# Splitting the rows of the first load of a max-pooling kernel into 8 KB pieces

## The chip, the cores and the metric

The kernel runs on one core of one Trainium2 chip. The metric is the device time of one execution in microseconds (us), lower is better. A time is a median over runs; a profile is one further execution, recorded by the hardware profiler.

## The reference

The input `x` has the shape (32, 256, 4096) in float32, and the output has 256 values for each of the 32 x 256 rows. As 4096 is divisible by 256, this is a maximum over every 16 neighbouring elements:

```python
for i in range(output_size):          # output_size = 256
    start = int(i * length / output_size)
    end = int((i + 1) * length / output_size)
    result[:, :, i] = np.max(x[:, :, start:end], axis=-1)
```

It reads 134.2 MB and writes 8.4 MB. There is one comparison for each element read and nothing else to compute.

## The kernel before

The kernel sees `x` as a list of 2,097,152 windows of 16 floats (64 bytes). The windows are dealt to the 128 partitions in two contiguous groups: group a gives each partition 15,436 windows that follow each other in memory, group b another 948. Within a group, partition p holds one unbroken stretch, so one load takes one contiguous row from each partition's stretch: a load of 1,024 windows is 128 rows of 64 KB.

The loads, in the order in which SyncE (SP) issues them:

- load 0, 1,024 windows a partition (8.4 MB, line 96): "the long first load";
- a load of 128 windows (`FIRST`, 1 MB in 128 rows of 8 KB, line 87), which has no number of its own;
- loads 1 to 13, 1,024 windows each (line 96);
- load 14 with 972 windows and load 15, which is group b, with 948 (line 96).

All loads go to one queue (q1), whose packets are carried by sixteen DMA engines; each load of 128 rows gives each engine eight rows. In the profile a row is one packet, and each engine adds one small packet at the end of a transfer for its completion.

The buffer `ring` holds two slots of 1,024 + 152 windows (`CHUNK` and `GAP`). Even loads go to the first slot, odd loads to the second, and within its slot every second load is moved up by 152 windows:

```python
low = n_loads % 2 * (CHUNK + GAP)
moved = n_loads // 2 % 2
at = low + moved * GAP
nc.sync.dma_start(out=ring[:, at * W : (at + n) * W], in_=xn)
```

So load 0 lies at windows 0 to 1,023, the 128-window load in 1,024 to 1,151, load 1 at 1,176 to 2,199, load 2 at 152 to 1,175, load 3 at 1,328 to 2,351, load 4 at 0 to 1,023 again. VectorE (DVE) reduces each load with `reduce_max` (helper `pooled`, line 56) in two parts: first the 872 windows that the slot's next load will overwrite, then the other 152. The next load into that slot can be issued when the part of 872 is done. Load 2 is the exception: it lies over the 128-window load's place too, so it waits for three reductions, of 872, 152 and 128 windows. VectorE works in the order of the program.

The framework places the waits: SP waits, before each issue from load 2 on, for the reduction that frees the place, and VectorE waits for each load's landing. SP issues in the order of the program, so an issue that waits holds up those behind it.

The results of group a gather in `kept` and are stored once, at the end, by SP (line 116). The last load's results overwrite a part of `ring` and are stored by ScalarE's queue (q10, line 113).

Of the kernel before, what the change touches and what calls it, by code (L numbers as in the profile page):

```python
# [1 line left out]

# [4 lines left out]


@with_exitstack
def kernel(  # L10
    ctx: ExitStack,
    tc: tile.TileContext,
    x: bass.AP,
    output_size: bass.AP,
    out: bass.AP,
):

    nc = tc.nc
    P = nc.NUM_PARTITIONS
    fp32 = mybir.dt.float32

    B, C, L = x.shape
    O = int(output_size)  # L30
    assert L % O == 0, (L, O)
    W = L // O
    total = B * C * O // P
    assert B * C * O % P == 0

    CHUNK = 1024
    GAP = 152
    FIRST = 128
    LOADS = 14

    last = 948
    group_a = [total - last - LOADS * CHUNK - FIRST] + [CHUNK] * LOADS
    group_a.insert(-1, FIRST)
    group_b = [last]
    assert FIRST < group_a[0] <= CHUNK and last * (W + 1) <= CHUNK * W

    pool = ctx.enter_context(tc.tile_pool(name="pool", bufs=1))
    ring = pool.tile([P, 2 * (CHUNK + GAP) * W], fp32, tag="ring", name="ring")
    kept = pool.tile([P, total - last], fp32, tag="kept", name="kept")

    xw = x.flatten_outer_dims().rearrange("r (o w) -> (r o) w", w=W)
    ow = out.flatten_outer_dims().rearrange("r o -> (r o)")

    def pooled(dst, at, n):

        nc.vector.reduce_max(  # L56
            out=dst,
            in_=ring[:, at * W : (at + n) * W].rearrange("p (n w) -> p n w", w=W),
            axis=mybir.AxisListType.X,
        )  # L60

    taken = 0

    def group(n):

        nonlocal taken
        span = slice(taken * P, (taken + n) * P)
        taken += n
        return (
            xw[span].rearrange("(p n) w -> p (n w)", p=P),  # L70
            ow[span].rearrange("(p n) -> p n", p=P),
        )

    stores = []
    n_loads = 0
    base = 0
    for g, loads in enumerate((group_a, group_b)):
        xg, og = group(sum(loads))
        a = sum(loads) if g == 0 else 0
        for n in loads[::-1]:  # L80
            if g == 0:
                a -= n
            xn = xg[:, a * W : (a + n) * W]
            dst = kept[:, base + a : base + a + n] if n != last else None
            if n == FIRST:

                nc.sync.dma_start(  # L87
                    out=ring[:, CHUNK * W : (CHUNK + n) * W], in_=xn
                )
                pooled(dst, CHUNK, n)  # L90
            else:

                low = n_loads % 2 * (CHUNK + GAP)
                moved = n_loads // 2 % 2
                at = low + moved * GAP
                nc.sync.dma_start(out=ring[:, at * W : (at + n) * W], in_=xn)  # L96
                if n != last:
                    cut = CHUNK - GAP if moved else GAP
                    parts = [(0, cut), (cut, n)]
                    for u, v in parts if moved else parts[::-1]:  # L100
                        pooled(dst[:, u:v], at + u, v - u)
                else:
                    end = (at + CHUNK) * W
                    last_kept = ring[:, end - n : end]
                    pooled(last_kept, at, n)
                n_loads += 1
            if g:
                a += n
        if g == 0:
            stores.append((og, kept[:, :]))  # L110
    assert taken == total

    nc.scalar.dma_start(out=og, in_=last_kept)
    tc.no_sync_barrier()
    for dst, src in stores:
        nc.sync.dma_start(out=dst, in_=src)


# [1 line left out]
_INS = ['x', 'output_size']  # L120
_OUTS = [((32, 256, 256), 'float32')]

_NUMBERS = {'output_size': 256}


# [26 lines left out]
```

## Time and profile before

| what | value |
|---|---|
| median of 3 runs | 337.88 us (337.59 to 338.27) |
| time of the profiled execution | 338.23 us |
| its span, first to last instruction | 336.4 us |
| busy time of VectorE | 276.5 us, 82% of the span |
| packets on the load queue q1 | 2,592, 142.12 MB, 98.2% of sixteen engines' span |
| mean DMA rate over the span | 424 GB/s |
| full reduction of 872 windows | 14.7 us, 15 times |
| issue of load 0 | at 0.73 us, takes 0.37 |
| issue of the 128-window load, of load 1 | at 1.15 us (0.43), at 1.62 us (0.42) |
| issue of load 2 | at 42.30 us, takes 0.33 |

The span is the time from the first to the last instruction; the execution's own time is 1.8 us longer, for what lies around it. All start times are counted from the start of the span. In a timeline line the columns are the start, the duration, the engine and line, the operation, output and input, and in brackets the engine's idle time before and what ended it; neighbouring instructions are merged into one line (x2, x3). In a table of windows the columns are the stretch, its length, VectorE's busy time, GpSimd's busy time, the granted clock, the DMA share and GB/s. A packet counts in the window in which it starts, with its whole duration and all its bytes. Therefore the share of a short window can be above 1, and the number and the mean duration of the packets that start in it can be worked out.

### The profile page before, as it was taken

The page shows a single profiled execution, that of the slowest core. Times are in us where ns is not written, and L with a number is a line of the kernel's source. Part 1 is how long each engine was busy: PE and PEld are TensorE (multiplying, and loading weights), DVE is VectorE, ACT ScalarE, POOL GpSimd, SP SyncE. Part 2 cuts the span into 40 slices and gives each one's busy share as a digit, 9 for nine tenths or more (in the row PEclk, how much of TensorE's full clock was granted, in tenths as well). Part 3 has the DMA queues.
Part 4 walks back from the last instruction along what each step waited for, and adds up shares of the span by engine and source line. Part 5 has one row for each costly group of instructions (what it writes and reads, how often), then busy time and mean ns, then how long its engine had stood idle before and what let it go on. Part 6 is the DMA issues. An engine that isn't in the chain of part 4 may idle for free.

```text
span 336.4 us, 112 instructions
## 1 busy us (share of the span) xinstructions
DVE 276.5 (82%) x32; POOL 0.2 (0%) x4
## 2 busy tenths in 40 slices
DVE  0029979499897979899797979979797997989794
POOL 0000000000000000000000000000000000000000
DMA  9898989999999999999999999999999999999997
GB/s 374 382 491 374 499 335 421 444 429 436 429 444 421 444 413 421 452 413 444 413 452 421 452 421 429 444 413 460 413 460 397 475 396 451 444 405 433 424 396 293
DMA packets 2736, 142.61 MB, mean 424 GB/s; under 512 B 304, under 2 KB 304, under 8 KB 432
## 3 DMA queue, kind: packets, MB, share of 16 engines
q1 hardware_dynamic: 2592, 142.12, 98.2%
q10 hardware_dynamic: 144, 0.49, 0.5%
HBM read 134.22 MB, written 8.39 MB: 424 GB/s over the span
## 4 chain that ended last, share of the span: by engine, by line
DMA 63%; DVE 35%; SPq 0%; issue 0%; DVEq 0%
DMA ring<-in_x_dram 63%; DVE kept L56 31%; DVE ring L56 5%; SPq L87 0%; SPq L96 0%; DVEq L56 0%
## 5 line engine op out<-in xcount | busy, mean ns | idle before, releaser
L56 DVE TENSOR_REDUCE kept<-ring 128x872 f32<-128x13952 f32 (+3 forms) x31 | 260.5, 8446 | 53.6 <-DMA ring<-in_x_dram 53.6
L56 DVE TENSOR_REDUCE ring<-ring 128x948 f32<-128x15168 f32 x1 | 16.0, 15953 | 1.9 <-DMA ring<-in_x_dram 1.9
L133 POOL MEMSET const-bfloat16-1.0<- 128x1 bf16 x1 | 0.1, 102 | 0.0
L133 POOL MEMSET const-uint8-127<- 128x1 uint8 x1 | 0.1, 102 | 0.0
L133 POOL MEMSET const-float32-0.0<- 128x1 f32 x1 | 0.1, 99 | 0.2 <-issue 0.2
L133 POOL MEMSET const-float32-1.0<- 128x1 f32 x1 | 0.1, 99 | 0.0
## 6 DMA issues: line engine op xcount, KB each, us to landing
ring<-in_x_dram SPq DMA_DIRECT2D x1, 7776.0 KB, 23.0
out_dram<-kept SPq DMA_DIRECT2D x1, 7718.0 KB, 20.0
ring<-in_x_dram SPq DMA_DIRECT2D x1, 7584.0 KB, 21.9
ring<-in_x_dram SPq DMA_DIRECT2D x1, 1024.0 KB, 24.1
out_dram<-ring ACTq DMA_DIRECT2D x1, 474.0 KB, 3.6
ring<-in_x_dram SPq DMA_DIRECT2D x14, 24.0
```

The costliest lines, as they stand in the source:

```text
L56: nc.vector.reduce_max(out=dst, in_=ring[:, at * W : (at + n) * W].rearrange("p (n w) -> p n w", w=W), axis=mybir.AxisListType.X,)
L133: nc = _bacc.Bacc("TRN2", target_bir_lowering=False, num_devices=1)
```

## The change

Load 0 alone is issued with a limit of 8,192 bytes on the piece that one descriptor moves. Its 128 rows of 64 KB become 1,024 pieces of 8 KB; in the built program the transfer's pattern is 128x8x2048 elements instead of 128x16384. Source, destination, order of issue, waits and all other loads are the same.

```diff
@@ -36,6 +36,7 @@
     CHUNK = 1024
     GAP = 152
     FIRST = 128
+    PIECE = 8192
     LOADS = 14
 
     last = 948
@@ -93,7 +94,11 @@
                 low = n_loads % 2 * (CHUNK + GAP)
                 moved = n_loads // 2 % 2
                 at = low + moved * GAP
-                nc.sync.dma_start(out=ring[:, at * W : (at + n) * W], in_=xn)
+                nc.sync.dma_start(
+                    out=ring[:, at * W : (at + n) * W],
+                    in_=xn,
+                    max_dma_last_dim=None if n_loads else PIECE,
+                )
                 if n != last:
                     cut = CHUNK - GAP if moved else GAP
                     parts = [(0, cut), (cut, n)]
```

## The prediction

> **What bounds the kernel now.** I read the page first. One engine works, VectorE, and the chain that ended last belongs to the transfers for 63% and to VectorE for 35%; the DMA line stands at nine tenths in nearly every slice.
>
> ```profile
> span 336.4 us, 112 instructions
> DVE 276.5 (82%) x32; POOL 0.2 (0%) x4
> ...
> q1 hardware_dynamic: 2592, 142.12, 98.2%
> ...
> DMA 63%; DVE 35%; SPq 0%; issue 0%; DVEq 0%
> ```
>
> So the sixteen DMA engines are the bound, and only three things can move the end: the rate at which they carry the loads, the time until they start, and holes in their stream. The timeline of VectorE shows where holes are: each line is the reductions of one load, and the bracket is the wait for that load to land.
>
> ```profile
> 22.80 19.47 DVE L56 TENSOR_REDUCE kept<-ring 128x872 f32<-128x13952 f32 x3 [22.80 <-DMA ring<-in_x_dram]
> 44.61 17.28 DVE L56 TENSOR_REDUCE kept<-ring 128x872 f32<-128x13952 f32 x2 [2.34 <-DMA ring<-in_x_dram]
> 66.21 17.28 DVE L56 TENSOR_REDUCE kept<-ring 128x872 f32<-128x13952 f32 x2 [4.32 <-DMA ring<-in_x_dram]
> 85.55 17.28 DVE L56 TENSOR_REDUCE kept<-ring 128x872 f32<-128x13952 f32 x2 [2.06 <-DMA ring<-in_x_dram]
> 104.91 17.28 DVE L56 TENSOR_REDUCE kept<-ring 128x872 f32<-128x13952 f32 x2 [2.08 <-DMA ring<-in_x_dram]
> ```
>
> Full loads land 19.34 us apart (66.21 to 85.55, 85.55 to 104.91 gives 19.36). Only load 2 is late: 44.61 to 66.21 is 21.60, so 2.26 us are lost there, once. The reason is its issue. It writes over the first load and over the 128-window load, so SP issues it only after the third reduction, at 42.30, just 2.3 us before load 1 has landed; load 4 is issued at 100.26, 4.65 us before load 3 lands. Windows over the packets (a packet counts where it starts; GB/s times the window over 65,536 bytes is the number of rows) show the hole:
>
> ```profile
> 4.50:4.70 0.20, 0.00 (x0) 0.00 (x0) 1.00 0.79 328
> ...
> 5.30:5.60 0.30, 0.00 (x0) 0.00 (x0) 1.00 1.01 437
> ...
> 40.90:41.80 0.90, 0.90 (x1) 0.00 (x0) 1.00 2.69 1165
> 43.30:44.30 1.00, 0.00 (x0) 0.00 (x0) 1.00 1.49 590
> 44.30:45.90 1.60, 1.29 (x1) 0.00 (x0) 1.00 0.80 287
> ```
>
> The last sixteen rows of load 1 start between 40.9 and 41.8 and take 2.42 each (2.69 x 0.9 x 16 / 16), so the engines run dry between 43.3 and 44.2. Nine engines take up load 2 by 44.3, seven only between 44.3 and 45.9. The landing waits for the last of them. The 0.9 us between the engines' ends dates from the start of the run: the first engine begins its second row at 4.5 to 4.7, the last two at 5.3 to 5.6.
>
> **The change, part by part.** *The first load's packets.* Removed are 128 rows of 64 KB, added 1,024 pieces of 8 KB: 64 for each DMA engine instead of 8. The 128-window load already consists of 8 KB rows. It lands at 1.15 + 24.1 = 25.25, 2.45 us after the first load, for 1 MB; an eighth of a full load's 19.34 is 2.42. Eight times the 0.03 is +0.26 us. The windows bound it: 79 packets start in 22.50 to 24.00, one every 0.304 us per engine, against 0.302 for an eighth of a 2.42 us row, +0.1 for 64 of them; by the 0.310 each takes (share 1.02 x 1.5 x 16 / 79) it is +0.5. I take +0.3, with +0.1 and +0.5 as ends. It is on the path: the first load's landing starts the reductions (14.69, 2.6 and 2.3 us back to back), which issue load 2, and the same engines carry the 128-window load and load 1 behind it. All shift together, so the lead of load 2's issue is unchanged by this term.
>
> *The issue.* SP's issue of the first load takes 0.37 us, then 0.43 and 0.42 for the two queued behind it on SP, the 128-window load and load 1. If all of it went with the descriptors, eightfold would be 2.9 us. Nothing waits for these two loads before the first has landed at 22.80, and SP itself has nothing else until 25.3, so some 20 us cover the delay on SP. What has no cover is the start of the first load on its last engine. The nearest row is the final store: sixteen rows for idle or nearly idle engines, fifteen of them starting within 314.90 to 315.10. If these 0.2 us are descriptors made one engine after another (9 each, the completion included), 65 each make 1.4 us, and the last engine starts 1.2 later; if they are something per engine, nothing is added. Ends: 0 and +1.2 us, and by the 0.37 us row at worst +2.6. I take 0, since the store's starts lie so close together that neither is proved, and keep +1.0 for the rival.
>
> *The first rows' wait.* The sixteen first rows, starting between 1.7 and 2.5, take 3.15 us each on average (share 3.94 over 0.8 us), 0.73 more than a row in the stream, and unevenly: that makes the 0.9 us of spread. Here sixteen requests of 64 KB meet at once. With pieces, each engine asks for 8 KB first. No row shows a cold start with 8 KB, so this is bounded: at best the excess of the late engines goes (-0.7 us on the first landing), at worst it stays, or every engine waits more than once (+0.7). I take an evener start and a landing about where it was.
>
> *Load 2's hole.* An engine has load 2's rows in time if they arrive before it runs dry. At the start, nothing begins within 1.0 us of the issue (0.73; the window 1.50 to 1.70 is empty) and all have begun by 2.5, so rows arrive 1.0 to 1.8 after an issue; for load 2 that is 43.3 to 44.1, exactly where the engines run dry. As the issue follows the *last* engine of the first load and running dry follows *each* engine, an early engine's lead is 1.9 us less its head start. If the start's spread falls from 0.9 to 0.4 or less, or if the two loads behind the first are held back half a microsecond by its longer issue, all or nearly all engines get through without stopping. Then up to 2.26 come back; I take 2.1, as some engine may still stop briefly. What is late next? Load 3 is issued at 59.32 either way (44.61 + 14.7), and load 2 would land at about 64.0, a lead of 4.6 us like the 4.65 of load 4: no new wait, and the 2.1 reach the end.
>
> Sum against the profiled execution of 338.23 us (span 336.4 and 1.8 around it): +0.3 - 2.1 = -1.8, so 336.4; that execution stands 0.35 above the median of 337.88, which gives 336.1 for a median.
>
> **Two rules of the skill.** The Trainium skill, "DMA: Bandwidth & Descriptors", section "Latency and other measured facts", gives about 0.6 us to the first byte for such a queue. By it load 2's rows arrive at 42.9, before any engine is dry; there would be no hole to close and the sum would be +0.3, or 338.2. The trace has nothing within 1.0 us of the first issue and seven engines stopped at 44.3, so I go by the trace. The same skill's "Perfetto Trace Analysis", section "What 'DMA-bound' means", speaks against the change: large descriptors matter where DMA engines or the issuing sequencer are the limit. It gives no price there; the sum by such a rule is the slower rival below.
>
> **The rivals.** *Nothing moves but the pieces' cost.* Spread and hole stay: 337.88 + 0.3 = 338.2. For it: the reads run over the same addresses in the same order, and the spread may come from the first access itself. Against it: 16 engines are so near the edge (nine in time, seven not) that a few tenths either way change the count. It takes 0.2 of the chance. "No change" means within 0.2%, 0.7 us here, about what a measurement of this kernel can tell.
>
> *The last engine starts later.* The longer list of descriptors starts the engines one after another: the first landing, and with it load 2's issue, moves by 0.3 + 1.0 us, while early engines run dry hardly later than now, so the hole stays and its end moves with the issue: 337.88 + 1.3 = 339.2, up to 340.8 by the worst row. It decides from 0.4 us of added start on the last engine (0.3 + 0.4 = 0.7). For it: the first three issues, of 0.37 to 0.43, are already longer than the 0.33 of the later ones, as if the making of descriptors were still busy with the one before; against it, the store's fifteen starts in 0.2 us. Chance 0.35.
>
> *The pieces are not made.* If the packets stayed 64 KB, the time would be 337.9; but the built program carries the first load as 128x8x2048, so 0.03.
>
> **How the numbers follow.** The hole closing has 0.42 of the chance, and its own range is 335.4 (all 2.26 back, the landing 0.5 earlier, +0.3) to 337.1 (1.1 of the hole back). It is likeliest because the hole is the one place where 2 us hang on tenths, and the present state is its bad side. Faster is 0.42, no change 0.23 (0.2 + 0.03), slower 0.35. As cases of both signs hold the chance, the range goes from 335.4 over the rivals to 339.6, which leaves out the worst issue.
>
> **What would show it.** In the profile after: about 2,592 + 896 packets on q1; the first reductions starting at 22.4 to 23.1; load 2 landing 19.3 to 19.8 us after load 1 with a wait near 2.1 instead of 4.32; all sixteen engines on load 2 by 44.5. If load 2 still lands 21 us after load 1, the hole stayed and I am wrong on the main step. If the first reduction starts after 23.5, the slower rival holds. If full loads stop landing 19.34 apart later on, something is at work that I don't see.

## The result, and the profile after

The changed kernel takes 338.83 us (median of 19 runs, 337.99 to 339.67), the kernel before 338.08 (19 runs, 337.37 to 338.88): a ratio of 1.0022, with a 95% interval of 1.0013 to 1.0031, so 0.75 us slower (0.4 to 1.0). I had forecast 336.1 and faster. The time lies inside the stated range only because that range spans the slower rivals too; the direction is wrong.

The page of the changed kernel shows that the pieces are there, 896 packets more on the load queue:

```profile
span 337.6 us, 112 instructions
...
q1 hardware_dynamic: 3488, 142.12, 98.2%
```

Its timeline of VectorE:

```profile
23.57 19.47 DVE L57 TENSOR_REDUCE kept<-ring 128x872 f32<-128x13952 f32 x3 [23.57 <-DMA ring<-in_x_dram]
45.41 17.28 DVE L57 TENSOR_REDUCE kept<-ring 128x872 f32<-128x13952 f32 x2 [2.37 <-DMA ring<-in_x_dram]
67.20 17.28 DVE L57 TENSOR_REDUCE kept<-ring 128x872 f32<-128x13952 f32 x2 [4.52 <-DMA ring<-in_x_dram]
86.58 17.28 DVE L57 TENSOR_REDUCE kept<-ring 128x872 f32<-128x13952 f32 x2 [2.09 <-DMA ring<-in_x_dram]
```

Against before, load 0 lands 0.77 us later, load 1 0.80, load 2 0.99, load 3 1.03, and the spans differ by 1.2 (this profiled execution took 339.39 us, 0.56 above its median). So two thirds of it is there with the first load, 0.2 more comes with load 2, and all of it is carried to the end. The hole at load 2 has not closed: 45.41 to 67.20 is 21.79 us against 19.38 for the next load, 2.41 us lost instead of 2.26. SP's issues show why:

```profile
0.73 0.41 SPq L97 DMA_DIRECT2D ring<-in_x_dram  x1
1.19 0.57 SPq L88 DMA_DIRECT2D ring<-in_x_dram  x1
1.81 0.42 SPq L97 DMA_DIRECT2D ring<-in_x_dram  x1
...
43.07 0.33 SPq L97 DMA_DIRECT2D ring<-in_x_dram  x1
```

Load 2 is issued at 43.07, later by the same 0.77 as the first landing, and load 1 lands later by 0.80: the lead is 2.34 us, before it was 2.31. In the windows over the packets (stretch, length, VectorE, GpSimd, clock, DMA share, GB/s) the engines' ends are as far apart as they were:

```profile
41.50:42.50 1.00, 1.00 (x1) 0.00 (x0) 1.00 2.42 1049
44.00:45.00 1.00, 0.00 (x0) 0.00 (x0) 1.00 2.13 721
45.00:46.90 1.90, 1.49 (x1) 0.00 (x0) 1.00 0.53 172
```

The last sixteen rows of load 1 (1,049 GB/s x 1.0 us / 65,536 bytes, the first line) need a window of 1.0 us, where 0.9 held them before. Eleven engines begin load 2 by 45.0, the other five only between 45.0 and 46.9.

### The profile page after: what moved, and what is told of

It reads as the page before. It is cut to its first block, busy times and chain, and to the rows that moved or that the text cites. A ratio compares the mean times of both kernels' runs of the same rounds, so it can differ in the third digit from the quotient of the medians.

```text
span 337.6 us, 112 instructions
## 1 busy us (share of the span) xinstructions
DVE 276.5 (82%) x32; POOL 0.2 (0%) x4
## 4 chain that ended last, share of the span: by engine, by line
DMA 63%; DVE 35%; SPq 0%; issue 0%; DVEq 0%
DMA ring<-in_x_dram 63%; DVE kept L57 30%; DVE ring L57 5%; SPq L88 0%; SPq L97 0%; DVEq L57 0%
```

## The experiments

Three questions were open: what the pieces cost and where, whether the hole is made by load 2's late issue, and how much earlier that issue would have to be.

**The hole by itself.** In the kernel before, the reduction of the 128-window load is put ahead of load 0's part of 152 windows (`parts` is walked as before; the second part of load 0 is only put off):

```diff
                 pooled(dst, CHUNK, n)            # the 128-window load
+                pooled(*later)                   # load 0's 152 windows
...
                     for u, v in parts if moved else parts[::-1]:
+                        if n_loads == 0 and u == 0:
+                            later = (dst[:, u:v], at + u, v - u)
+                            continue
                         pooled(dst[:, u:v], at + u, v - u)
```

> The kernel before, with two reductions exchanged: the one of the 128-window load is done ahead of load 0's part of 152 windows, so load 2, which lies over the 872 windows and over the 128-window load's place, can be issued some 2.6 us earlier, at about 39.7 instead of 42.3. Theory 'hole by the late issue': no DMA engine runs dry, load 2 lands 19.3 to 19.4 us after load 1 (21.6 before), and the time falls by 2.2 us to about 335.8. Rival 'hole by something else' (the memory is slow for load 2 whenever it comes): load 2 still lands 21 us or more after load 1, and the time stays at 338.1.

It took 335.95 us (335.82 to 336.08), 0.9929 of before (0.9915 to 0.9943). SP issues load 2 at 39.72, VectorE has no wait of 4.32 any more, and load 2 lands 19.34 us after load 1:

```profile
39.72 0.33 SPq L97 DMA_DIRECT2D ring<-in_x_dram  x1
...
22.81 19.47 DVE L56 TENSOR_REDUCE kept<-ring 128x872 f32<-128x13952 f32 x3 [22.81 <-DMA ring<-in_x_dram]
44.63 17.28 DVE L56 TENSOR_REDUCE kept<-ring 128x872 f32<-128x13952 f32 x2 [2.35 <-DMA ring<-in_x_dram]
63.97 17.28 DVE L56 TENSOR_REDUCE kept<-ring 128x872 f32<-128x13952 f32 x2 [2.06 <-DMA ring<-in_x_dram]
```

The late issue makes the hole. The spread of the runs falls too, from 1.4 us in the nine runs of before beside it to 0.3 in five, which makes this order the better base for measuring small prices.

**The pieces without the hole.** The same edit in the changed kernel.

> The changed kernel with the same exchange of reductions. Theory 'stream': the pieces cost time in the transfers themselves, and as the stream of loads bounds the kernel with or without the hole, this is 0.75 us above the exchanged kernel with whole rows: about 336.6. Rival 'issue of load 2': the pieces only shift the first landing and so load 2's issue; with the issue early, the extra time is hidden and this equals the exchanged kernel with whole rows, about 335.8 to 336.0.

It took 336.45 us (336.40 to 336.62), 0.50 above whole rows in the same order, and no run of one reaches the other. The price is in the transfers and is not hidden by an early issue; the rival that it acts through load 2's issue alone is out. The 0.50 is less than the 0.75 expected, but within the interval of that difference (0.4 to 1.0).

```profile
23.41 19.47 DVE L57 TENSOR_REDUCE kept<-ring 128x872 f32<-128x13952 f32 x3 [23.41 <-DMA ring<-in_x_dram]
45.24 17.28 DVE L57 TENSOR_REDUCE kept<-ring 128x872 f32<-128x13952 f32 x2 [2.36 <-DMA ring<-in_x_dram]
64.59 17.28 DVE L57 TENSOR_REDUCE kept<-ring 128x872 f32<-128x13952 f32 x2 [2.07 <-DMA ring<-in_x_dram]
```

All three are 0.60 to 0.62 us later than with whole rows.

**Pieces in every full load.** The limit is given to all loads of 1,024 windows, reductions in the old order.

```diff
-                    max_dma_last_dim=None if n_loads else PIECE,
+                    max_dma_last_dim=PIECE if n == CHUNK else None,
```

> 8 KB pieces in all fourteen loads of 1,024 windows, reductions in their old order. Theory 'two prices': in the stream a full load in pieces costs about 0.27 us more (427 to 429 GB/s between 5 and 20 us of the changed kernel's trace, against 65,536 bytes in 2.42 us on each of sixteen engines, 433 GB/s), and only the load that starts on idle engines pays another 0.45 us: 338.1 + 14 x 0.27 + 0.45, about 342.3. Rival 'one price': every load in pieces pays the 0.75 us measured for the first, 338.1 + 14 x 0.75, about 348.6.

It took 344.30 us (343.33 to 344.64), between the two forecasts. The profile gives the price cleanly:

```profile
45.77 17.28 DVE L57 TENSOR_REDUCE kept<-ring 128x872 f32<-128x13952 f32 x2 [2.90 <-DMA ring<-in_x_dram]
65.64 17.28 DVE L57 TENSOR_REDUCE kept<-ring 128x872 f32<-128x13952 f32 x2 [2.59 <-DMA ring<-in_x_dram]
85.52 17.28 DVE L57 TENSOR_REDUCE kept<-ring 128x872 f32<-128x13952 f32 x2 [2.60 <-DMA ring<-in_x_dram]
105.39 17.28 DVE L57 TENSOR_REDUCE kept<-ring 128x872 f32<-128x13952 f32 x2 [2.59 <-DMA ring<-in_x_dram]
```

Full loads land 19.87 to 19.88 us apart instead of 19.35: 0.53 us each, for 56 more pieces on each engine 9.4 ns a piece. Both theories had the wrong size, 0.27 and 0.75. This execution also shows no hole; with 335.95 + 14 x 0.53 it should take 343.4, and it took 343.33. It is the fastest of the five by 0.9 us. The other four, 344.27 to 344.64, would fit a hole such as the next run has, but none of them was profiled.

**Pieces in loads 1 to 13 only**, load 0 with whole rows.

```diff
-                    max_dma_last_dim=None if n_loads else PIECE,
+                    max_dma_last_dim=PIECE if n == CHUNK and n_loads else None,
```

> 8 KB pieces in loads 1 to 13, whole rows in load 0. Theory 'two prices': 338.1 + 13 x 0.27, about 341.6, and 0.7 us below the kernel with pieces in all fourteen. Rival 'one price': 338.1 + 13 x 0.75, about 347.8. If load 2's start on partly dry engines pays the price of a cold start too, 0.4 us more in either. In the trace the first landing is at 22.8 as before.

It took 344.25 us (343.73 to 344.69), again between the two forecasts, and not below the kernel with pieces in all loads. The first landing is at 22.83, as with whole rows. The hole is there again:

```profile
45.17 17.28 DVE L57 TENSOR_REDUCE kept<-ring 128x872 f32<-128x13952 f32 x2 [2.87 <-DMA ring<-in_x_dram]
66.95 17.28 DVE L57 TENSOR_REDUCE kept<-ring 128x872 f32<-128x13952 f32 x2 [4.50 <-DMA ring<-in_x_dram]
86.81 17.28 DVE L57 TENSOR_REDUCE kept<-ring 128x872 f32<-128x13952 f32 x2 [2.59 <-DMA ring<-in_x_dram]
```

21.78 us to load 2 against 19.86 to the next: 1.9 us lost. 335.95 + 13 x 0.53 + 1.9 is 344.7; the profiled execution took 344.40. As a test of load 0's own price it says nothing, because the hole moves by more than that. Why this profile has a hole and the last one has none is open. Load 1 is in pieces in both, and SP issues load 2 with nearly the same lead, at 42.90 with pieces in all loads (2.87 us before load 1's landing) and at 42.33 here (2.84):

```profile
42.90 0.38 SPq L97 DMA_DIRECT2D ring<-in_x_dram  x1
...
42.33 0.38 SPq L97 DMA_DIRECT2D ring<-in_x_dram  x1
```

**Piece sizes, without the hole.** The exchanged order with `PIECE` set to 32,768, 16,384 and 2,048.

> The exchanged order of reductions (no hole at load 2, so the times lie closely together), and load 0 in pieces of 32 KB: 16 for each engine instead of 8. Theory 'price for each piece': in the run with pieces in all loads, full loads land 19.88 us apart against 19.35, 0.53 us for 56 more pieces an engine, 9 ns each, and 4 ns in the first 30 or so; so 8 more cost 0.03 to 0.08 us: 336.0, the same as whole rows (335.95). Theory 'price of the start': if it is the first requests of idle engines in small pieces that cost, any division pays part of it: 336.1 to 336.3.

> As before with pieces of 16 KB, 32 for each engine. 'Price for each piece': 24 more pieces at 4 to 9 ns, 0.1 to 0.2 us: 336.05 to 336.15. 'Price of the start': 336.2 to 336.4, nearly what pieces of 8 KB gave (336.45).

> As before with pieces of 2 KB, 256 for each engine. 'Price for each piece': 248 more at 9 ns, 2.3 us: about 338.2. 'Price of the start': little more than with 8 KB, 336.5 to 337.

| pieces of load 0 | more pieces an engine | time, us (lowest to highest) | above whole rows | for each piece |
|---|---|---|---|---|
| whole rows, 64 KB | 0 | 335.95 (335.82 to 336.08) | | |
| 32 KB | 8 | 336.04 (335.79 to 336.16) | 0.09 | within the scatter |
| 16 KB | 24 | 336.19 (336.09 to 336.24) | 0.24 | 10 ns |
| 8 KB | 56 | 336.45 (336.40 to 336.62) | 0.50 | 9 ns |
| 2 KB | 248 | 338.35 (338.11 to 338.56) | 2.40 | 9.7 ns |

The extra time goes roughly with the number of pieces, and the forecast by pieces holds at 2 KB (2.3 expected). A price of the cold start alone would have given 336.5 to 337 there. It is not the pieces alone either: 336.19 with 16 KB lies between the two forecasts, and the next experiment's table shows a part that arises at the start. With 2 KB a wait on SP shows as well, in SP's lines of that profile:

```profile
0.73 0.42 SPq L98 DMA_DIRECT2D ring<-in_x_dram  x1
1.20 15.30 SPq L88 DMA_DIRECT2D ring<-in_x_dram  x1
16.55 0.63 SPq L98 DMA_DIRECT2D ring<-in_x_dram  x1
```

The 128-window load's issue behind the 4,096 pieces takes 15.30 us, and load 1 is issued only at 16.55. The first landing is at 25.40, so both are still in the queue in time; the next load lands 21.83 us after it, as with whole rows (21.82).

**Rows instead of pieces.** Load 0 as eight transfers of 128 windows, each with 128 rows of 8 KB, in the exchanged order.

```diff
-                nc.sync.dma_start(out=ring[:, at * W : (at + n) * W], in_=xn)
+                step = n if n_loads else 128
+                for j in range(0, n, step):
+                    nc.sync.dma_start(
+                        out=ring[:, (at + j) * W : (at + j + step) * W],
+                        in_=xn[:, j * W : (j + step) * W],
+                    )
```

> The exchanged order with load 0 as eight transfers of 128 windows, each with 128 rows of 8 KB, instead of one transfer with rows cut in pieces: the same number of 8 KB packets on each engine (64), in another order, and seven more completions. If the price is one for each packet, as with 8 KB pieces: about 336.5. If it comes from cutting a row inside one transfer, and separate rows cost the 0.03 us a MB that the 128-window load shows: 336.2.

It took 336.00 us (335.83 to 336.08), below both forecasts: 0.05 above whole rows and within their scatter, against 0.50 for pieces. But its packets are no cheaper. These are windows over the packets of load 0, the first two lines with 8 KB pieces in the exchanged order, the last two with eight transfers:

```profile
1.70:6.00 4.30, 0.00 (x0) 0.00 (x0) 1.00 0.96 341
6.00:21.00 15.00, 0.00 (x0) 0.00 (x0) 1.00 1.01 425
...
1.70:6.00 4.30, 0.00 (x0) 0.00 (x0) 1.00 1.00 375
6.00:21.00 15.00, 2.69 (x1) 0.00 (x0) 1.00 1.01 425
```

From 6.0 us on both move 425 GB/s. Whole rows of 2.42 us on sixteen engines make 433, so 15 us at 425 cost either of them about 0.3 us. The difference is made before: by 6.0 us 197 packets have begun with eight transfers and 179 with pieces (375 and 341 GB/s x 4.3 us / 8,192 bytes), a little over one more for each engine. The table counts each packet's bytes evenly over its duration in the trace, sums the sixteen engines, and gives how far they are behind whole rows in the exchanged order (a minus is ahead):

| profile | at 6.0 us | at 21.5 us |
|---|---|---|
| whole rows in load 0, four other profiles | -0.09 to 0.02 | -0.09 to 0.01 |
| 8 KB pieces: changed kernel, exchanged order, all loads | 0.18, 0.10, 0.21 | 0.49, 0.42, 0.51 |
| 16 KB pieces; 32 KB pieces | 0.09; 0.10 | 0.17; 0.12 |
| eight transfers of 8 KB rows | -0.22 | 0.07 |

So 8 KB packets cost 0.30 to 0.32 us between 6.0 and 21.5 us in either form. Pieces lose another 0.1 to 0.2 us at the start, and the eight transfers gain 0.2 there, which pays for most of their packets. It is one profile of them: their first reduction of 872 windows starts at 23.10, where whole rows have 22.74 to 22.93 and 8 KB pieces 23.39 to 23.57. Why the starts differ is open. The number of issues differs, and so may the order of the reads: with eight transfers an engine takes 8 KB of each of its eight rows before the next 8 KB of any; in which order it takes the pieces no view shows. One difference beside it: here the framework put load 0's 152 windows first of all, at 8.17, which frees load 2's place no later than the exchanged order does.

**How much lead closes the hole.** Whole rows; 30 or 60 of load 0's 152 windows are reduced after the 128-window load. The edit is shown against the exchanged order:

```diff
                         if n_loads == 0 and u == 0:
-                            later = (dst[:, u:v], at + u, v - u)
-                            continue
+                            later = (dst[:, :30], at, 30)     # 60 in the second run
+                            u = 30
                         pooled(dst[:, u:v], at + u, v - u)
```

> Whole rows in all loads; 30 of the 152 windows of load 0's second part are reduced after the 128-window load instead of before it, so load 2 is issued 0.5 us earlier (about 41.8), with a lead of 2.8 us over load 1's landing instead of 2.3. The prediction took half a microsecond of lead for enough. 'Half a microsecond closes the hole': load 2 lands 19.4 to 19.9 us after load 1, time 336.0 to 336.4. Rival 'the hole needs all engines in time': as in the run with pieces in loads 1 to 13, where a lead of 2.84 us left 1.9 us of hole, some engine still runs dry; load 2 lands 20.5 us or more after load 1, time 337.2 to 338.0.

> As before with 60 windows moved: load 2's issue 1.0 us earlier, a lead of 3.3 us. Rows arrive 1.0 to 1.8 us after an issue and the engines run dry 0.4 to 1.2 us before load 1's landing, so 3.3 us is more than the 1.8 + 1.2 that the latest row and the earliest engine need: the hole is closed in both views, load 2 lands 19.4 us after load 1, time 335.9 to 336.1. If the hole stays above 1 us (337 or more), arrival under load takes longer than the start shows.

They took 335.71 us (335.54 to 336.08) and 335.83 us (335.56 to 336.02), a little below the forecasts; load 2 lands 19.34 and 19.35 us after load 1. Half a microsecond is enough. SP's issue of load 2 and the windows over the packets with 30 windows moved, same stretches as in the prediction:

```profile
41.74 0.33 SPq L97 DMA_DIRECT2D ring<-in_x_dram  x1
...
40.90:41.80 0.90, 0.90 (x2) 0.00 (x0) 1.00 2.69 1165
43.30:44.30 1.00, 0.00 (x0) 0.00 (x0) 1.00 2.48 1049
44.30:45.90 1.60, 1.32 (x1) 0.00 (x0) 1.00 0.28 123
```

The engines' ends lie as they did before (the share and the rate of the first window are the same), but now all sixteen take up load 2 by 44.3 (1,049 x 1.0 / 65.5), the three packets after that being second rows. Load 2 is issued at 41.74 here, 1.7 us before the first engine runs dry at 43.40, against 1.1 before (42.30 and 43.36). The lead over load 1's landing is 2.84 us, the same with which the run with pieces in loads 1 to 13 still lost 1.9 us, while the profile with pieces in all loads lost nothing with 2.87. With pieces in loads 1 and 2 this lead is thus at the edge, and what decides there wasn't tried. These two and the exchanged order are equal within their scatter; each is faster than both kernels of this case, 0.9927 of before (0.9912 to 0.9942) with 30 windows moved.

## Why the prediction was wrong

**The pieces' price** was taken as +0.3 with +0.5 as its upper end; for one load without the hole it is 0.50 as the median. The term was worked out from the 128-window load's 2.45 us, and for load 0's packets in the stream it was about right: 0.30 to 0.32 between 6.0 and 21.5 us in the three profiles with 8 KB pieces, and as much with eight separate transfers. What is left is a loss of 0.1 to 0.2 at the start, which the sum had at nothing. In later loads a piece costs more, 0.53 for a load. That the bound by the packets' duration, +0.5, met the total is in part luck, since it held nothing for the start.

**The first rows' wait** is the step that turned the sign. I took an evener start, a spread of 0.4 us or less, with no row for it: the text itself said that no row shows a cold start with 8 KB. The trace after shows the ends of the engines 0.9 to 1.0 us apart, as before, and the start with pieces is slower and not evener. The first line is the changed kernel, the second the one with eight transfers:

```profile
1.70:3.00 1.30, 0.00 (x0) 0.00 (x0) 1.00 0.87 164
...
1.70:3.00 1.30, 0.00 (x0) 0.00 (x0) 1.00 0.97 271
```

By 3.0 us 26 pieces have begun, and they take 0.70 us each on average (0.87 x 1.3 x 16 / 26), where pieces in the stream take 0.31; with eight transfers it is 43 packets of 0.47. The views don't tell the engines apart, so whether one engine waited more than once is not separated. The first landing was 0.77, 0.60 and 0.58 late in three profiles with 8 KB pieces; the engines' mean lag of 0.4 to 0.5 is most of that.

**Load 2's hole** was read rightly in place, cause and size: an earlier issue takes away 2.1 to 2.6 us, and half a microsecond suffices, as the step said. What failed is that the change was to supply it. The prediction held the answer in its first term, "All shift together, so the lead of load 2's issue is unchanged by this term"; that is what happened, a lead of 2.34 after 2.31. The other way named for it, that the two loads behind the first would be held back by a longer issue, did not happen either: 0.41, 0.57 and 0.42 us of issue, all hidden by the first load, as even 15.30 us were with 2 KB. The step was also too short on when rows arrive: it took 1.0 to 1.8 us after an issue from the start of the run, but its own windows have seven engines beginning load 2 only 2.0 to 3.6 us after the issue at 42.30, and in the changed kernel five begin it 1.9 to 3.8 us after 43.07.

**The rivals.** "Nothing moves but the pieces' cost" had the mechanism and a chance of only 0.2; with 0.5 instead of 0.3 its 338.2 becomes 338.4, and 338.6 from the median of 19 runs of before. That leaves 0.25 of the measured 0.75, whose interval (0.4 to 1.0) holds 0.5 as well. In the two profiles the hole grew by 0.15 (2.26 to 2.41); I can't say more of it. The slower rival's mark, a first reduction after 23.5, was there at 23.57, but its mechanism wasn't: it needed the last engine to start 0.4 us or more later, and the engines' ends lie only 0.1 us further apart than before. Most of the price comes along the load, and loads that start on busy engines pay it too. Its sum of 339.2 came nearer by accident of size.

**The two rules.** By the Trainium skill, "DMA: Bandwidth & Descriptors", section "Latency and other measured facts" (0.6 us to the first byte), there should be no hole. Counted from the end of the first issue at 1.10 us the start of the run agrees, as the first row begins at 1.73; but with 1.1 us from load 2's issue to the first dry engine there was a hole, and with 1.7 us there was none, so the trace decided rightly. The rule of the Trainium skill in "Perfetto Trace Analysis", section "What 'DMA-bound' means", that large descriptors matter where the DMA engines are the limit, held: 0.53 us for a load, or 9.4 ns a piece, with 8 KB pieces in the stream.

## What to carry to other kernels

Where the DMA engines are the bound, as in this kernel, cut no rows of a transfer finer than needed: the price is small but is paid in full, since nothing hides it. Two forms that end at the same time need not cost the same on the way; look at the start and at the stream apart. A hole in a saturated stream is closed by the lead of the issue, so look for the instruction that releases it and move work behind that one; a change that delays the release and the stream alike leaves the hole as it is. A step whose only support is a bound should keep the sign that the costed terms have.

## What the runs showed of the hardware

A DMA engine that ran dry beside busy ones was slow to start again: 2.0 to 3.6 us after the issue in the kernel before and 1.9 to 3.8 in the changed one, against 1.0 to 1.8 on engines that were all idle at the start of the run. With whole rows, 1.1 us from the issue to the first dry engine cost 2.26 us of landing and 1.7 us cost nothing. With pieces in loads 1 and 2, 1.6 us cost 1.9 us in one profile and 1.7 us nothing in another, a difference too small to rest on.

The price of an 8 KB packet was not even along the stream. In the three profiles with 8 KB pieces in load 0 it takes 0.309 us on average between 6 and 12 us and 0.314 between 15 and 21; with eight transfers it is 0.309 until 15 us and 0.313 to 0.314 after 18. An eighth of a row of 2.42 us is 0.302. What changes there is open.
